# Top-k stage of a retrieval layer: a third of the subtractions on VectorE, transposes a token tile later, one-hots written in input order

## The chip, the cores and the metric

The kernel runs on one core of a Trainium2 chip. The metric is the device time of one execution in microseconds. Five engines work in parallel, each with its own queue that it takes strictly in order: TensorE (PE, matmuls; PEld is its weight load), VectorE (DVE), ScalarE (ACT), GpSimd (POOL) and SyncE (SP), which here only issues DMAs. They wait for one another by semaphores.

## The reference

A block of a small network on 256 tokens of width 1,024, in float32. Only its retrieval layer matters here: every token picks 128 of 16,384 experts (8 heads, top 16 of 256 candidates, which come from the top 16 of 128 sub-keys in each of two halves), and the outputs of the picked experts are summed by gate.

```python
def peer_ffn(xn, w_query, subkeys, u_tab, v_tab):
    q = (xt @ w_query).reshape(T, PEER_HEADS, 2, PEER_QDIM // 2)
    s = jnp.einsum('thpd,hpkd->thpk', q, subkeys).astype(jnp.float32)
    sv, si = lax.top_k(s, PEER_TOPK)
    cand = (sv[:, :, 0, :, None] + sv[:, :, 1, None, :]).reshape(T, PEER_HEADS, PEER_TOPK * PEER_TOPK)
    cand_id = (si[:, :, 0, :, None] * PEER_NKEYS + si[:, :, 1, None, :]).reshape(...)
    top_s, pos = lax.top_k(cand, PEER_TOPK)
    expert = jnp.take_along_axis(cand_id, pos, axis=-1)
    gate = jax.nn.softmax(top_s, axis=-1)
    def apply(args):
        ug, vg = u_tab[ec], v_tab[ec]
        act = jax.nn.gelu(jnp.einsum('thkd,td->thk', ug, xc).astype(jnp.float32), approximate=False)
        return jnp.einsum('thk,thkd->td', (gc * act).astype(vg.dtype), vg)
```

## The kernel before

Nothing is gathered. The kernel computes the activation of all 16,384 experts for all tokens, multiplies it with a dense matrix of gates, which is zero for experts not picked, and multiplies with the whole second table. So it streams both tables of 64 MB through TensorE.

**Weights.** Every product in float32 is made of three in a faster format. `wload` (L97 to 111) loads 128x1024 weights (`raw`, issued by SP), has ScalarE round them (`hi`, L106) and takes the rest `lo = raw - hi` (L109) on VectorE or GpSimd, as a pattern of letters says, which is walked round and round. There are 3 buffers of `raw`, 4 of `hi` and 4 of `lo`. `ws` (L242 to 262) then issues 24 matmuls for such a half: per block of 128 rows `hi` with the upper part of x (L255), `hi` with its lower part (L256) and `lo` with the upper part (L257). The 3rd matmul of a half is thus the first that wants its `lo`.

**Stages.** `peer` (L674 to 707) merges pairs of generators: it advances whichever has done the smaller share of its steps, so the number of steps that a generator announces sets how its instructions are written among those of the other. A scheduler then fixes the order on each engine. In the top-k stage `peer_topk` runs beside `peer_u` on the first half of the first table (64 halves, numbered from 0 here; pattern "G": every lo on GpSimd). For each tile of 128 tokens `peer_topk` computes the scores (16 products L749, recorded as 32), searches the 16 halves of heads (L755 to L759), makes candidates (L767), searches those of 8 heads (L772 to L776), and turns positions into expert numbers (L782 to L797: compare with 0..15, multiply, sum). Then come an Exp on ScalarE, the gate sums (L804 to L806) and three transposes on TensorE (L811 to L813), from which ScalarE makes `sel` and VectorE the copy `gate` (L815).

In the gates stage `peer_g` runs beside `peer_u` on the second half of the first table (pattern "VG"). For 8 tokens at a time VectorE compares the selected numbers with a ramp (`E`, L852, bf16, written as key x token), then for 4 tokens ScalarE copies one (`A`, L857) and VectorE multiplies the other by the gate (`B`, L858), both written as token x key in float32; 4 matmuls (L862, two records each) give the dense gates of 4 tokens, which multiply the activations there (L868) or are kept for later ones (L870). The last stage, `peer_v`, multiplies with the second table (L898), its lo's by the same pattern "VG".

Of the kernel before, what the change touches and what calls it, by code (L numbers as in the profile page):

```python
# [9 lines left out]
F32 = mybir.dt.float32  # L10
# [5 lines left out]
AF = mybir.ActivationFunctionType  # L16
ALU = mybir.AluOpType
AX = mybir.AxisListType
PSUM = bass.MemoryType.PSUM
P = 128  # L20
# [10 lines left out]
TOPK_STEPS = 90  # L31
# [14 lines left out]
class Net:  # L46
    def __init__(self, ctx, tc, T):
# [13 lines left out]
        self.u_pattern = "G"  # L61
# [667 lines left out]
    def peer_topk(self, qT, pool, sel, gate):  # L729
# [12 lines left out]
        nc.sync.dma_start(skT, T["subkeysT"])  # L742
        for tt in range(2):
# [9 lines left out]
            for hp in range(16):  # L753
                o, x = hp * 16, s[:, hp * P:(hp + 1) * P]
# [34 lines left out]
            for q in range(2):  # L789
# [7 lines left out]
                v.tensor_reduce(ij[:, q * P:(q + 1) * P], e3, axis=AX.X, op=ALU.add)  # L797
                yield

            self.tc.keep_in_program_order(a.activation(gt, gt, AF.Exp))  # L800
            for _ in range(2):
                yield
            sm = self.tiny.tile([P, 8], F32, tag="gsm", name=self.nm("gsm"))
            v.tensor_reduce(sm, g3, axis=AX.X, op=ALU.add)  # L804
            v.reciprocal(sm, sm)
            v.tensor_tensor(g3, g3, sm[:, :, None].to_broadcast([P, 8, 16]), op=ALU.mult)  # L806
            t = slice(tt * P, tt * P + P)
            for _ in range(2):
                yield
            p = self.sm_ps()  # L810
            nc.tensor.transpose(p[:, :P], ij[:, :P], self.ident)  # L811
            nc.tensor.transpose(p[:, P:2 * P], ij[:, P:], self.ident)
            nc.tensor.transpose(p[:, 2 * P:3 * P], gt, self.ident)  # L813
            a.activation(sel[:, :, t], p[:, :2 * P].rearrange("p (q t) -> p q t", q=2), AF.Copy)
            v.tensor_copy(gate[:, t], p[:, 2 * P:3 * P])  # L815

    def peer_u(self, xT, n0, n1):
# [16 lines left out]
        self.lo_pattern = self.u_pattern  # L834
        for x in g:
            yield x
            self.lo_pattern = self.u_pattern

    def peer_g(self, sel, gate, pool):
# [8 lines left out]
        for b in range(S // T1):  # L848
# [4 lines left out]
            for u in range(0, T1, T2):  # L853
                i = u // T2
                t0 = b * T1 + u
                A, B = [h[q].rearrange("p (n t j) -> p n t j", n=2, t=T2)[:, i] for q in range(2)]
                a.activation(A, E[0][:, :, u:u + T2].rearrange("p j t -> p t j"), AF.Copy)  # L857
                v.tensor_tensor(B, E[1][:, :, u:u + T2].rearrange("p j t -> p t j"),  # L858
                                gate[:, t0:t0 + T2, None].to_broadcast([P, T2, P]), op=ALU.mult)
                p = self.bank("sm").rearrange("p (t j) -> p t j", t=T2)  # L860
                for k in range(T2):
                    nc.tensor.matmul(p[:, k], A[:, k], B[:, k], start=True, stop=True)  # L862
# [618 lines left out]
```

## Time and profile before

| | |
|---|---|
| median of 3 runs | 1701.74 us (1701.32 to 1702.23) |
| the profiled execution | 1709.63 us, its span 1707.5 us, mean granted clock 0.985 |
| busy, share of the span | PE 97%, DVE 70%, ACT 55%, POOL 25% |
| top-k stage | 195 to 400 us |
| gates stage | 400 to 641 us |
| last product and end of the layer | 641 to 1010 us |

What stands outside 195 to 1010 us is the attention block ahead and two more layers behind. Busy TensorE records overlap and their ends are modelled, so the distance from one start to the next is the better measure of its pace. The clock is a share of full speed.

### The profile page before, as it was taken

To read this page: it belongs to the slowest core of one execution; us is meant where nothing else is said; L and a number is where in the kernel's file an instruction comes from. 1 tells how busy PE (TensorE), PEld (TensorE's weight loads), DVE (VectorE), ACT (ScalarE), POOL (GpSimd) and SP (SyncE) were. 2 spreads that over 40 slices of the span, in tenths; PEclk is the share of its full clock that TensorE was granted. 3 is DMA by queue.
4 is the path that set the end of the run, shared out by engine and by line. 5 is a ranking of instruction groups with operands and counts; after the bars stand their busy time and mean duration, and the time that the engine had idled before them with its cause. 6 is when DMAs were issued, how large, how long until landed. Compare 5 with 4: busy or idle time off the path is not lost.

```text
span 1707.5 us, 27637 instructions
## 1 busy us (share of the span) xinstructions
PE 1648.9 (97%) x10592; PEld 1467.1 (86%) x10592; DVE 1191.3 (70%) x2236; ACT 947.1 (55%) x1435; POOL 429.4 (25%) x191
## 2 busy tenths in 40 slices
PE   6999999989999999999999999989999989999998
PEld 5878999989999997888888879869998777799986
DVE  7766597915999995444444468878884685688845
ACT  4545545446676665555555557466664455566634
POOL 1000498974333334444444411100000000000000
PEclk9999999999999999999999999999999998999999
DMA  7424655555444446556755665436666642366661
GB/s 268 158 75 153 201 165 162 161 171 163 137 136 148 129 147 205 186 187 215 226 186 186 189 184 173 124 114 198 187 190 186 208 161 66 112 192 189 192 188 62
DMA packets 83200, 285.07 MB, mean 167 GB/s; under 512 B 10556, under 2 KB 14589, under 8 KB 82941
## 3 DMA queue, kind: packets, MB, share of 16 engines
q1 hardware_dynamic: 83068, 283.31, 53.4%
q8 instruction: 83, 1.36, 0.3%
q14 instruction: 49, 0.39, 0.1%
HBM read 281.16 MB, written 2.12 MB: 166 GB/s over the span
## 4 chain that ended last, share of the span: by engine, by line
PE 71%; DVE 23%; ACT 2%; issue 2%; DMA 1%; POOL 1%; SPq 0%; DVEq 0%; ACTq 0%; POOLq 0%
PE mm L898 20%; PE mm L256 9%; PE mm L257 9%; PE mm L255 9%; PE mm L196 6%; PE mm L198 6%; PE mm L197 6%; DVE h L858 6%; DVE lo L109 4%; DVE E L852 3%; DVE act L868 2%; PE sm L553 1%; PE sm L525 1%; DVE xn L322 1%; PE sm L334 1%
## 5 line engine op out<-in xcount | busy, mean ns | idle before, releaser
L106 ACT ACTIVATE hi<-raw 128x1024 fp32r<-128x1024 f32 x513 | 542.7, 1060 | 380.7 <-PE mm L256 141.4
L109 DVE TENSOR_TENSOR lo<-raw,hi 128x1024 fp32r<-128x1024 f32 x353 | 433.9, 1231 | 192.2 <-ACT hi L106 183.1
L255 PE MATMUL mm<-xTh,hi 128*128 128x256 f32 x1992 | 564.0, 283 | 0.1
L257 PE MATMUL mm<-xTh,lo 128*128 128x256 f32 x1992 | 557.0, 280 | 4.9 <-POOL lo L109 4.9
L256 PE MATMUL mm<-xTl,hi 128*128 128x256 f32 x1992 | 557.4, 280 | 0.4 <-DVE xTl L289 0.4
L109 POOL TENSOR_TENSOR lo<-raw,hi 128x1024 fp32r<-128x1024 f32 x160 | 405.7, 2541 | 426.4 <-ACT hi L106 416.7
L257 PEld LDWEIGHTS mm<-xTh,lo 128*128 128x128 f32 x1992 | 375.7, 189 | 6.1 <-POOL lo L109 5.9
L255 PEld LDWEIGHTS mm<-xTh,hi 128*128 128x128 f32 x1992 | 375.8, 189 | 1.3 <-issue 0.6
L256 PEld LDWEIGHTS mm<-xTl,hi 128*128 128x128 f32 x1992 | 375.9, 189 | 0.9 <-DVE xTl L289 0.7
L858 DVE TENSOR_TENSOR h<-E,gate 128x512 f32<-128x512 bf16 x64 | 115.2, 1800 | 4.2 <-PE sm L862 4.2
L196 PE MATMUL mm<-hi,xTh 128*128 128x512 f32 x256 | 107.6, 421 | 2.0 <-DVE xTl L289 1.0
L198 PE MATMUL mm<-hi,xTl 128*128 128x512 f32 x256 | 104.1, 408 | 2.2 <-DVE xTl L289 2.2
L197 PE MATMUL mm<-lo,xTh 128*128 128x512 f32 x256 | 104.7, 409 | 0.2 <-DVE lo L109 0.2
L289 DVE TENSOR_TENSOR xTl<-act,xTh 128x256 fp32r<-128x256 f32 x64 | 45.1, 713 | 80.3 <-PE mm L898 78.8
L289 DVE TENSOR_TENSOR wl<-act,wh 128x256 fp32r<-128x256 f32 x64 | 42.8, 675 | 82.9 <-PE mm L898 82.9
L857 ACT ACTIVATE h<-E 128x512 f32<-128x512 bf16 x64 | 73.1, 1143 | 40.9 <-DVE E L852 39.3
L1313 DVE SCALAR_TENSOR_TENSOR fc<-mm,cw,fc 128x255 f32<-128x255 f32 (+1 forms) x176 | 84.4, 480 | 3.1
L898 PE MATMUL mm<-hi,xTh 128*128 128x512 f32 x256 | 80.7, 396 | 0.9 <-DVE act L828 0.9
L898 PE MATMUL mm<-hi,xTl 128*128 128x512 f32 x256 | 80.6, 396 | 0.8 <-DVE xTl L289 0.8
L898 PE MATMUL mm<-lo,xTh 128*128 128x512 f32 x256 | 80.5, 395 | 0.0
L898 PE MATMUL mm<-hi,wl 128*128 128x512 f32 x256 | 80.2, 395 | 0.0
L898 PE MATMUL mm<-hi,wh 128*128 128x512 f32 x256 | 80.2, 395 | 0.0
(298 smaller groups left out, 2398.3 us busy)
## 6 DMA issues: line engine op xcount, KB each, us to landing
raw<-in_peer_uT SPq DMA_DIRECT2D x128, 512.0 KB, 3.7
raw<-in_peer_v SPq DMA_DIRECT2D x128, 512.0 KB, 4.4
raw<-in_ffn_up_ws SPq DMA_DIRECT2D x88, 512.0 KB, 4.3
raw<-in_ffn_down_a SPq DMA_DIRECT2D x40, 512.0 KB, 4.5
raw<-in_w_in_xs SPq DMA_DIRECT2D x20, 512.0 KB, 4.8
raw<-in_ab_ws SPq DMA_DIRECT2D x16, 512.0 KB, 4.5
raw<-in_ple_gate_xs SPq DMA_DIRECT2D x16, 512.0 KB, 4.3
raw<-in_w_query_ws SPq DMA_DIRECT2D x12, 512.0 KB, 5.0
```

Source lines behind the costliest of these rows:

```text
L106: nc.scalar.activation(hi, raw, AF.Copy)
L109: eng.tensor_tensor(lo, raw, f32(hi), op=ALU.subtract)
L196: nc.tensor.matmul(p, xh[:, k, t], hi[:, w], start=n == 1 and kk == 0, stop=False)
L197: nc.tensor.matmul(p, xh[:, k, t], lo[:, w], start=False, stop=False)
L198: nc.tensor.matmul(p, xl[:, k, t], hi[:, w], start=False, stop=n == total[c] and kk == 1)
L255: nc.tensor.matmul(o, hi[:, w], xh[:, k, :], start=k == 0, stop=False)
L256: nc.tensor.matmul(o, hi[:, w], xl[:, k, :], start=False, stop=False)
L257: nc.tensor.matmul(o, lo[:, w], xh[:, k, :], start=False, stop=k == 7)
L289: self.nc.vector.tensor_tensor(dl, p, f32(dh), op=ALU.subtract)
L858: v.tensor_tensor(B, E[1][:, :, u:u + T2].rearrange("p j t -> p t j"), gate[:, t0:t0 + T2, None].to_broadcast([P, T2, P]), op=ALU.mult)
L898: nc.tensor.matmul(self.acc[tt][c], st_[:, t], mv[:, c * 512:c * 512 + 512], start=first and j == js[0] and i == 0, stop=j == last and i == 2)
L1313: v.scalar_tensor_tensor(c[:, o + sft:o + S], p[:, o:o + S - sft], cw[:, wi, j:j + 1], c[:, o + sft:o + S], op0=ALU.mult, op1=ALU.add)
```

## The change

There are five parts. The lines from L31 on move by one or more, so the same operation has other line numbers behind the change: lo L110, the three matmuls of a half L256 to L258, score products L763, L792, L795 and L797 are L808, L811 and L813, transposes L753, `E` L857, `A` L863, `B` L864, gate products L867, last product L903.

1. The gate sums, the transposes and the copies behind them become a function `finish`. For tile 0 it is called in the middle of tile 1's search (at the 7th of 16), for tile 1 after 14 more steps. The Exp is issued after the first sum. The top-k stage announces 74 steps instead of 90.
2. The pattern of the top-k stage is "GGV": the lo's of halves 1, 4, 7, ..., 61 are VectorE's.
3. `A` and `B` are written in the order in which `E` lies. `A` keeps its place as token x key, so ScalarE writes in steps of 512 bytes; `B` becomes key x token, so that TensorE reads the moving operand of L867 in steps of 16 bytes.
4. Once 96 of the 128 blocks of activations are done, in the second half of the gates stage, the pattern is "VGG" instead of "VG".
5. `peer_u` leaves the pattern at "V", so the last product has all its lo's on VectorE.

```diff
-TOPK_STEPS = 90
+TOPK_STEPS = 74
+TOPK_REST = 14
-        self.u_pattern = "G"
+        self.u_pattern = "GGV"
+        def finish(tt, ij, gt, g3):
+            sm = self.tiny.tile([P, 8], F32, tag="gsm", name=self.nm("gsm"))
+            v.tensor_reduce(sm, g3, axis=AX.X, op=ALU.add)
+            v.reciprocal(sm, sm)
+            v.tensor_tensor(g3, g3, sm[:, :, None].to_broadcast([P, 8, 16]), op=ALU.mult)
+            p = self.sm_ps()
+            for i, x in enumerate((ij[:, :P], ij[:, P:], gt)):
+                self.tc.keep_in_program_order(nc.tensor.transpose(p[:, i * P:(i + 1) * P], x, self.ident))
+            t = slice(tt * P, tt * P + P)
+            a.activation(sel[:, :, t], p[:, :2 * P].rearrange("p (q t) -> p q t", q=2), AF.Copy)
+            v.tensor_copy(gate[:, t], p[:, 2 * P:3 * P])
...
             for hp in range(16):
+                if tt and hp == 6:
+                    finish(0, *late)
...
                 v.tensor_reduce(ij[:, q * P:(q + 1) * P], e3, axis=AX.X, op=ALU.add)
+                if not q:
+                    self.tc.keep_in_program_order(a.activation(gt, gt, AF.Exp))
                 yield
-            self.tc.keep_in_program_order(a.activation(gt, gt, AF.Exp))
...
+            late = ij, gt, g3
+        for _ in range(TOPK_REST):
+            yield
+        finish(1, *late)
...
-        self.lo_pattern = self.u_pattern
         for x in g:
+            self.lo_pattern = "VGG" if gates and self.done[0] >= 96 else self.u_pattern
             yield x
-            self.lo_pattern = self.u_pattern
+        self.lo_pattern = "V"
...
-                A, B = [h[q].rearrange("p (n t j) -> p n t j", n=2, t=T2)[:, i] for q in range(2)]
-                a.activation(A, E[0][:, :, u:u + T2].rearrange("p j t -> p t j"), AF.Copy)
-                v.tensor_tensor(B, E[1][:, :, u:u + T2].rearrange("p j t -> p t j"),
-                                gate[:, t0:t0 + T2, None].to_broadcast([P, T2, P]), op=ALU.mult)
+                A = h[0].rearrange("p (n t j) -> p n j t", n=2, t=T2)[:, i]
+                B = h[1].rearrange("p (n j t) -> p n j t", n=2, t=T2)[:, i]
+                a.activation(A, E[0][:, :, u:u + T2], AF.Copy)
+                v.tensor_tensor(B, E[1][:, :, u:u + T2], gate[:, None, t0:t0 + T2].to_broadcast([P, P, T2]), op=ALU.mult)
...
-                    nc.tensor.matmul(p[:, k], A[:, k], B[:, k], start=True, stop=True)
+                    nc.tensor.matmul(p[:, k], A[:, :, k], B[:, :, k], start=True, stop=True)
```

VectorE's queue at the end of tile 0, before: the last search, the comparison with 0..15 for both numbers, the multiplications and the sums.

```order
L776 MAX_INDEX small_2406<-small_2405,big_2403 128x8 x2
L782 TENSOR_TENSOR small_2634<-small_2405 128x128
L785 TENSOR_SCALAR small_2636<-small_2406 128x128
L786 TENSOR_SCALAR small_2636<-small_2406 128x128
L788 CAST small_2639<-small_2636 128x256
L792 TENSOR_TENSOR big_2641<-small_2639,io_1918 128x2048
L792 TENSOR_TENSOR big_2682<-small_2639,io_1918 128x2048
L795 TENSOR_TENSOR big_2641<-big_2641,small_2401 128x2048
L795 TENSOR_TENSOR big_2682<-big_2682,small_2401 128x2048
L797 TENSOR_REDUCE small_2633<-big_2641 128x128
L797 TENSOR_REDUCE small_2633<-big_2682 128x128
L804 TENSOR_REDUCE gsm_2774<-small_2634 128x8
```

The same place now, where lo_2550 is that of half 16, lo_2628 of half 19, and the next two of halves 22 and 25.

```order
L798 TENSOR_TENSOR small_2733<-small_2467 128x128
L804 CAST small_2738<-small_2735 128x256
L808 TENSOR_TENSOR big_2740<-small_2738,io_1918 128x2048
L808 TENSOR_TENSOR big_2807<-small_2738,io_1918 128x2048
L110 TENSOR_TENSOR lo_2550<-raw_2547,hi_2549 128x1024
L811 TENSOR_TENSOR big_2740<-big_2740,small_2463 128x2048
L811 TENSOR_TENSOR big_2807<-big_2807,small_2463 128x2048
L813 TENSOR_REDUCE small_2732<-big_2740 128x128
L110 TENSOR_TENSOR lo_2628<-raw_2625,hi_2627 128x1024
L813 TENSOR_REDUCE small_2732<-big_2807 128x128
L110 TENSOR_TENSOR lo_2774<-raw_2771,hi_2773 128x1024
L110 TENSOR_TENSOR lo_2846<-raw_2843,hi_2845 128x1024
```

Subtractions that had not been in this queue now stand between the operations of the top-k stage. In tile 1 they stand the same way: VectorE's queue there now, with lo_3474 that of half 40, lo_3552 of half 43 and lo_3698 of half 46 (those of halves 31, 34 and 37 stand among the searches).

```order
L857 TENSOR_TENSOR E_4277<-sel,iota 128x1024
L804 CAST small_3662<-small_3659 128x256
L864 TENSOR_TENSOR h_79<-E_4277,gate 128x512
L808 TENSOR_TENSOR big_3664<-small_3662,io_1918 128x2048
L110 TENSOR_TENSOR lo_3474<-raw_3471,hi_3473 128x1024
L811 TENSOR_TENSOR big_3664<-big_3664,small_3424 128x2048
L808 TENSOR_TENSOR big_3731<-small_3662,io_1918 128x2048
L813 TENSOR_REDUCE small_3656<-big_3664 128x128
L110 TENSOR_TENSOR lo_3552<-raw_3549,hi_3551 128x1024
L811 TENSOR_TENSOR big_3731<-big_3731,small_3424 128x2048
L864 TENSOR_TENSOR h_79<-E_4277,gate 128x512
L813 TENSOR_REDUCE small_3656<-big_3731 128x128
```

Behind the last row two more `E` and the lo of half 46 follow. On TensorE, before, the transposes of tile 0 and the score products of tile 1 stood together after half 22.

```order
L257 MATMUL mm_2778<-xTh_70,lo_2782 128x256
L811 MATMUL sm_2815<-ident,small_2633 128x128
L812 MATMUL sm_2815<-ident,small_2633 128x128
L813 MATMUL sm_2815<-ident,small_2634 128x128
L749 MATMUL sm_2822<-big_1920,qT_1436 128x128 x4
L749 MATMUL sm_2828<-big_1920,qT_1436 128x128 x4
```

Now the score products of tile 1 stand after half 24 and the transposes of tile 0 after half 29, as below; those of tile 1 stood after half 45 and stand after half 60.

```order
L258 MATMUL mm_3012<-xTh_70,lo_3022 128x256
L753 MATMUL sm_3083<-ident,small_2732 128x128 x2
L753 MATMUL sm_3083<-ident,small_2733 128x128
L256 MATMUL mm_3094<-xTh_70,hi_3097 128x256
L257 MATMUL mm_3094<-xTl_71,hi_3097 128x256
```

The transposes have moved away from the products that they stood ahead of, and back by 7 and by 15 halves.

## Rows read from the trace of the kernel before

**Rows 1.** Stages: window, its length, busy (x instructions) by engine, granted clock, DMA.

```profile
core 0: us, PE busy (x) PEld busy (x) DVE busy (x) ACT busy (x) POOL busy (x), PEclk, DMA share, GB/s
195.00:400.00 205.00, 192.34 (x1610) 190.89 (x1610) 139.35 (x423) 97.04 (x115) 173.19 (x64) 0.98 0.55 167
400.00:512.00 112.00, 112.00 (x971) 112.00 (x969) 104.02 (x145) 78.09 (x118) 35.04 (x16) 1.00 0.45 138
512.00:640.00 128.00, 127.14 (x1072) 124.67 (x1071) 127.75 (x165) 84.17 (x134) 40.25 (x17) 1.00 0.46 141
641.00:1010.00 369.00, 365.24 (x1564) 293.53 (x1563) 180.02 (x233) 195.30 (x273) 153.71 (x68) 1.00 0.63 196
```

**Rows 2.** What TensorE waited for, 195 to 400 us: total, times, longest.

```profile
PE sm L813 <- DVE small L806: 5.3, 1, 5.3
PE mm L257 <- POOL lo L109: 4.9, 5, 1.3
PE sm L749 <- DVE gate L815: 2.5, 1, 2.5
```

**Rows 3.** A window behind the longest of them, columns as in rows 1.

```profile
345.80:352.60 6.80, 5.80 (x27) 5.81 (x28) 1.23 (x2) 1.33 (x4) 3.17 (x2) 0.50 0.63 204
```

**Rows 4.** TensorE's timeline, start of the top-k stage: start, duration, operation.

```profile
195.28 3.73 PE L749 MATMUL sm<-big,qT 128*128 128x128 f32 x32
...
199.08 0.28 PE L257 MATMUL mm<-xTh,lo 128*128 128x256 f32 x1
...
201.88 0.28 PE L257 MATMUL mm<-xTh,lo 128*128 128x256 f32 x1
```

**Rows 5.** VectorE's timeline in the gates stage.

```profile
557.72 2.97 DVE L858 TENSOR_TENSOR h<-E,gate 128x512 f32<-128x512 bf16 x1
560.60 1.29 DVE L852 TENSOR_TENSOR E<-sel,iota 128x1024 bf16<-128x1024 bf16 x2
...
562.55 1.06 DVE L858 TENSOR_TENSOR h<-E,gate 128x512 f32<-128x512 bf16 x1
...
563.77 1.22 DVE L109 TENSOR_TENSOR lo<-raw,hi 128x1024 fp32r<-128x1024 f32 x1
```

**Rows 6.** VectorE's timeline in the top-k stage, tile 0.

```profile
198.06 0.49 DVE L755 MAX8 small<-big 128x8 f32<-128x128 f32 x2 [10.87 <-ACT big L751]
...
216.77 2.28 DVE L767 TENSOR_TENSOR big<-small 128x2048 f32<-128x2048 f32 x1
218.96 0.29 DVE L762 CAST small<-small 128x256 f32<-128x256 uint32 x1
...
235.06 2.38 DVE L788 CAST small<-small 128x256 f32<-128x256 uint32 x1
237.47 8.90 DVE L792 TENSOR_TENSOR big<-small,io 128x2048 f32<-128x2048 f32 x2
246.29 8.88 DVE L795 TENSOR_TENSOR big<-big,small 128x2048 f32<-128x2048 f32 x2
255.09 4.47 DVE L797 TENSOR_REDUCE small<-big 128x128 f32<-128x2048 f32 x2
```

**Rows 7.** GpSimd by line, 240 to 262 us, then 400 to 641: busy, mean ns, idle.

```profile
L109 POOL TENSOR_TENSOR lo<-raw,hi 128x1024 fp32r<-128x1024 f32 x6 | 22.0, 3707 | 0.3 <-ACT hi L106 0.3
...
L109 POOL TENSOR_TENSOR lo<-raw,hi 128x1024 fp32r<-128x1024 f32 x33 | 79.2, 2400 | 168.6 <-ACT hi L106 159.2 <-PE mm L257 5.2 <-ACT act L870 4.2
```

**Rows 8.** By line, 400 to 641; line L830 (min/median/max ns); a VectorE row of 646 us.

```profile
L857 ACT ACTIVATE h<-E 128x512 f32<-128x512 bf16 x62 | 70.9, 1143 | 38.7 <-DVE E L852 37.1 <-PE mm L257 1.6
...
L862 PE MATMUL sm<-h,h 128*128 128x128 f32 x512 | 68.6, 277 | 0.9 <-DVE h L858 0.3
...
L830 ACT ACTIVATE act<-mm x63: 186/577/618, 207.0 to 639.5; 128x512 f32<-128x512 f32 x32, 128x496 f32<-128x496 f32 x1, 128x480 f32<-128x480 f32 x1, 128x464 f32<-128x464 f32 x1
...
646.12 0.68 DVE L828 TENSOR_TENSOR act<-mm,act 128x512 f32<-128x512 f32 x1
```

**Rows 9.** What TensorE waited for, 536 to 650 us.

```profile
PE mm L898 <- DVE act L828: 0.9, 1, 0.9
PE mm L898 <- DVE xTl L289: 0.8, 1, 0.8
```

More of the change, by code (lines that the diff above doesn't have):

```diff
@@ L797, in peer_topk @@
                 v.tensor_reduce(ij[:, q * P:(q + 1) * P], e3, axis=AX.X, op=ALU.add)
+                if not q:
+                    self.tc.keep_in_program_order(a.activation(gt, gt, AF.Exp))
                 yield
-            self.tc.keep_in_program_order(a.activation(gt, gt, AF.Exp))
[L801 to L815, printed above, removed]
+            late = ij, gt, g3
+        for _ in range(TOPK_REST):
+            yield
+        finish(1, *late)
     def peer_u(self, xT, n0, n1):
```

## Prediction

> **What bounds the kernel now.** I read the busy time by stage first, then what TensorE waited for, then the timelines of the engines that it waited for. Four stages matter, and TensorE is busy nearly all the time in each [rows 1]: the top-k stage (195 to 400 us: 192.34 of 205), the gates stage in two parts (112.00 of 112, then 127.14 of 128), and the last product (365.24 of 369). So work that leaves VectorE, ScalarE or GpSimd is worth only the time that TensorE waits, and work that arrives there costs nothing until TensorE has to wait for it. In the top-k stage it waits 12.7 us in all: 5.3 for a transpose (L813) whose input VectorE has not written, 4.9 in five waits for a lo that GpSimd is late with, 2.5 for the gate copy that holds a PSUM bank [rows 2]. The long stop has a sequel: for 6.80 us after it the granted clock is 0.50, the lower level, with TensorE busy 5.80 of them [rows 3], so about 2.9 us more are lost. The change can win at most 15.6 us here.
>
> **Pace of the top-k stage.** TensorE takes 2.80 us for a half of 1,024 weight columns, from one first use of lo to the next (199.08 to 201.88), and 0.117 us for each of the 32 records of a score product (3.73 us); the first product starts at 195.28 [rows 4]. I count the halves of this stage from 0: half n wants its lo at 199.08 + 2.80n, plus whatever was waited.
>
> **Part 1: gate sums and transposes later.** The operations are the same. The transposes of tile 0 now stand after half 29 and those of tile 1 after half 60 in TensorE's queue, where VectorE has written their inputs long before, and the score products of tile 1 no longer stand behind the gate copy. That removes 5.3 + 2.5 + 2.9 = 10.7 us. Next late in their place are the lo's.
>
> **Part 2: every third lo of the top-k stage on VectorE.** 21 of 64 leave GpSimd. The cost is not 21 x 1.22 us [rows 5] but where they stand: VectorE is an in-order queue and top-k fills it. Before, nothing that TensorE wants half by half was in that queue.
>
> Tile 0: VectorE starts at 198.06 and finishes its two L792 at 246.29 (the start of L795) [rows 6], and in the new order the lo's of halves 4, 7, 10 and 13 stand ahead of that point and that of half 16 right behind it. Its lo is ready at 246.29 + 5 x 1.22 = 252.4 and wanted at 199.08 + 16 x 2.80 = 243.9: 8.5 us late. That is with the durations of before, and those contain GpSimd. L792 and L795 take 4.45 each, two operands in SBUF and 2,048 elements, where L767 of the same size took 2.28 [rows 6]; beside them GpSimd's lo took 3.71 instead of 2.40 [rows 7]. They take turns. So the lower end has L792 at 2.28 (-4.3) and the cast L788 at 0.29 as L762 instead of 2.38 (-2.1): 2.1 us late. For half 19, two L795, one L797 (half of 4.47) and a lo come next: 8.0 us alone or 12.4 as before, against 8.4 of three halves. By the end of tile 0 TensorE has waited 2.1 to 12.5 us.
>
> Tile 1: VectorE starts 2.78 us after the first score product [rows 4, 6], and half 25 wants its lo 3.80 us after it. Half 40 wants its lo 15 halves and three transposes later, at 3.80 + 42.0 + 0.35 = 46.2. Ahead of it stand the 16 sub-key searches (18.71), L767 (2.19), the gate copy and a cast (0.3 each), the candidate searches up to L788 (235.06 - 218.96 = 16.1), two E at 0.65, one gated one-hot at 1.06 [rows 5], an L792 (2.28) and four lo's with its own (4.9): 2.78 + 47.1 = 49.9, 3.7 late. With L788 and L792 as before it is 8.0. Half 43 takes L795, L792, L797 and lo (8.0 to 12.4) and half 46 L795, L797, a gated one-hot, two E and lo (8.1 to 12.2), each against 8.4. So TensorE waits 3.7 to 15.8 us in tile 1.
>
> Together 5.8 to 28.3. Where between depends on how often VectorE meets GpSimd. GpSimd keeps two of three subtractions, so I take two thirds of the way, 20.8, and 1.2 for meetings of the new lo's themselves (ten of them, each 0 to 2.2 more; up to 2 at the upper end): 22. A stop of more than 5 us is likely once, with its slow clock after it as in [rows 3]: 3 more (0 to 6). The stage: 22 + 3 - 12.7 - 2.9 = **+9.4**; ends -10 and +21.
>
> **Part 3: one-hots in input order.** ScalarE's copy reads E with a stride of 16 bytes and takes 1.14 us, where a copy of 512 elements in a row takes 0.58 [rows 8]; VectorE's multiplication takes 1.06, where L828 on 512 takes 0.68 [rows 5, 8]. So about 0.4 us per four tokens leave VectorE, and some 0.5 ScalarE, if ScalarE's spread write is free. What they bring is TensorE's waiting only: 0 of 112 and 0.86 of 128 us [rows 1], with small slips between products, 2 at most. The price of the other side, a moving operand read at a stride of 16 bytes, no row shows. Its lower bound is 0, since the columns are as many; its upper bound is the rival below. I take 0: the record of 128 columns takes 0.117 us, 0.9 ns a column, half the pace at which L257 takes its 256 columns (0.117 too) [rows 4], so there is room.
>
> The Trainium skill, "SBUF - State Buffer", section Specifications, has 16-byte lines in SBUF and asks for two hits on a line for full bandwidth. That speaks for the change on ScalarE and VectorE, as these rows do, and against it on TensorE, whose every column is now a new line; the sum would be +9 without that penalty and that of the second rival with it.
>
> **Part 4: second half of the gates stage, two thirds of its lo's to GpSimd.** VectorE there is busy 127.75 of 128 us [rows 1], but part of that is waiting: the same multiplication takes 2.97 or 1.06 us [rows 5] by whether a GpSimd lo stands in its way. It loses a third of a lo per period and gains a third of a meeting. With part 3: 0, between -2 and +4.
>
> **Part 5: all lo's of the last product on VectorE.** 64 more, 78 us, in a stage where it is busy 180.02 of 369 and TensorE is never short of work [rows 1]: 0, hidden by the products; uncovered it would be 78. At the switch TensorE waits 0.9 and 0.8 us for VectorE [rows 9]; I take half a microsecond off that (0 to 1.7).
>
> **Sum.** 9.4 + 0 - 0.5 = +8.9 us. The profiled execution takes 1709.63 us, of which 1707.5 is the span, and would become 1718.5. The median of the runs shown is 1701.74, 7.9 below it, and the sum carries over as it stands: 1710.7.
>
> **Rivals.**
> First, **faster: VectorE hardly meets GpSimd any more.** Then the durations alone hold: 5.8 us of new waits, no slow clock, against 15.6 gone, 2 from the gates and 1.7 at the switch: -13.5, 1688 us. For it: L767 met nothing at 2.28, and two thirds of the subtractions are two thirds of the meetings at most. Against it: GpSimd was busy 21.92 of 22.00 us beside L792 and L795 (six at 3.71) [rows 7], and its remaining lo's come just there. Between this and my forecast the sums cancel, at 1702.
> Second, **slower still: TensorE pays for the stride.** Per element the strided reads of [rows 5, 8] cost 0.74 ns more on VectorE and 1.1 on ScalarE. On 128 columns and 512 records [rows 8] that is 49 to 72 us, all on a bound engine: 1760 to 1783 with the rest. It decides as soon as one column takes more than the 0.9 ns it has. For it: both engines that read so show it. Against it: none of them is TensorE.
> Third, the change **doesn't do what it says**: the transposes still wait. Against that stand 15 halves, 42 us, by which tile 1's move back; I give it nothing of its own.
>
> **Chances.** Forecast (new waits eat the gain, 1705 to 1726): 0.40. Cancelling, within 0.2%, which is about what a measurement of this kernel can tell from no change: 0.16. Faster, 1688 to 1698: 0.29. Stride on TensorE: 0.15. So faster 0.29, same 0.16, slower 0.55. The range leaves out the last case and the tails: 1688 to 1726, the upper end being 28.3 + 2 + 6 - 15.6 + 4 = +25. Cases of both signs hold much of the chance; the forecast's own range is 1705 to 1726.
>
> **What would show it.** In the changed profile: no wait of a transpose for VectorE; waits of L258 for VectorE's lo at halves 16, 19, 40, 43 and 46, some 20 us, perhaps with the clock at 0.50 behind one. L808 and L811 (L792, L795 now) at 2.3 us would be the first rival, records of the gate product above 0.117 us the second. The copy near 0.6 and the multiplication near 0.7 us would confirm part 3. I am wrong if the top-k stage comes out shorter than 205 us.

## The result, and the profile of the changed kernel

The changed kernel takes 1757.89 us (median of 6 runs) against 1701.99 of the kernel before (also 6): 1.0324 times as long, with an interval from 1.0304 to 1.0344. Slower, as forecast, but by 56 us where 9 were forecast, and outside the range. It is the second rival, to which the prediction gave 0.15.

The stages by TensorE's starts show where the time is. The top-k stage runs from the first score product to the first gate product, the gates stage to the last gate product.

| us | before | after | difference |
|---|---|---|---|
| top-k stage | 204.7 | 207.1 | +2.4 |
| gates stage | 238.4 | 294.3 | +55.9 |
| switch, last product | 362.9 | 360.7 | -2.2 |
| the rest | 901.5 | 896.7 | -4.8 |
| span | 1707.5 | 1758.8 | +51.3 |

The rest holds the same work in both. It begins up to 6 us earlier or later from run to run of any of the kernels here, and nothing is made of it.

The windows of the changed kernel, with the columns of [rows 1]: the top-k stage, then 230 us of the gates stage.

```profile
195.00:400.00 205.00, 191.22 (x1581) 189.66 (x1581) 143.20 (x429) 94.77 (x112) 115.69 (x42) 0.97 0.50 163
...
470.00:700.00 230.00, 230.00 (x1576) 221.48 (x1576) 154.82 (x244) 130.53 (x204) 68.30 (x29) 1.00 0.37 120
```

TensorE is busy all of those 230 us, and VectorE only 154.82, where before it was busy 127.75 of 128 [rows 1]. Nothing keeps TensorE waiting there (the list of its waits, below, has none in this stage), so TensorE itself is slower. Its timeline shows at what: start, duration and operation around one step of four tokens.

```profile
522.93 0.28 PE L258 MATMUL mm<-xTh,lo 128*128 128x256 f32 x1
523.05 1.98 PE L867 MATMUL sm<-h,h 128*128 128x128 f32 x8
524.66 0.48 PE L256 MATMUL mm<-xTh,hi 128*128 128x256 f32 x1
524.98 0.28 PE L257 MATMUL mm<-xTl,hi 128*128 128x256 f32 x1
```

The same place in the kernel before:

```profile
556.88 1.05 PE L862 MATMUL sm<-h,h 128*128 128x128 f32 x8
557.69 0.36 PE L255 MATMUL mm<-xTh,hi 128*128 128x256 f32 x1
557.89 0.28 PE L256 MATMUL mm<-xTl,hi 128*128 128x256 f32 x1
```

From the first record of a step to the second matmul behind it passes 1.93 us instead of 1.01. The ends of records are modelled, so this distance of starts is what counts; the median of all 64 steps is 1.935 against 1.013. The added 0.922 us on 64 steps are 59.0 us (57.8 when the 64 steps are added up one by one), and the stage grew by 55.9. Where the other 2 to 3 us were saved stays open: before, the list of waits has only 0.3 us in this stage. The start-to-start distance of two records rose from 0.112 to 0.227 us in the median.

The groups of the changed kernel (busy, mean ns of one, idle before) answer to [rows 8]:

```profile
L867 PE MATMUL sm<-h,h 128*128 128x128 f32 x512 | 126.5, 403 | 0.0
...
L863 ACT ACTIVATE h<-E 128x512 f32<-128x512 bf16 x64 | 74.2, 1162 | 49.1 <-PE sm L867 41.3
```

ScalarE's copy did not get cheaper: 1.162 us against 1.143. It now reads in runs of four and writes in steps of 512 bytes. VectorE's multiplication did, to 0.679 us at its fastest (line L864: minimum, median and maximum of 64).

```profile
L864 DVE TENSOR_TENSOR h<-E,gate x64: 679/1493/2316, 319.6 to 683.7; 128x512 f32<-128x512 bf16 x64
```

From 195 to 720 us TensorE's waits are these, all of them in the top-k stage; they answer to [rows 2]:

```profile
PE mm L258 <- DVE lo L110: 10.0, 5, 5.6
PE mm L258 <- POOL lo L110: 3.5, 1, 3.5
PE mm L256 <- ACT hi L107: 0.3, 1, 0.3
```

The transposes and the gate copy hold nothing up any more, and VectorE's lo's do, as forecast, for half as long. The slow clock has not gone: it comes twice, from within the stop of 5.6 us on and around that of 3.5 us (columns as in [rows 3]).

```profile
244.10:250.80 6.70, 3.76 (x17) 3.76 (x18) 6.70 (x3) 0.00 (x0) 1.80 (x1) 0.50 0.41 109
329.40:336.10 6.70, 5.82 (x27) 5.82 (x28) 6.70 (x4) 0.00 (x0) 4.18 (x2) 0.50 0.39 133
```

Half of TensorE's busy time in them, as the prediction reckoned it, is 4.8 us, against 2.9 before. Waits of 13.8 and these 4.8, less the 12.7 and 2.9 of before, give +3.0 us for the stage; it measured +2.4.

### The profile page after: what moved, and what is told of

It is laid out like the page before. It is cut to its first block, busy times and chain, and to the rows that moved or that the text cites. A ratio compares the mean times of both kernels' runs of the same rounds, so it can differ in the third digit from the quotient of the medians.

```text
span 1758.8 us, 27633 instructions
## 1 busy us (share of the span) xinstructions
PE 1702.5 (97%) x10592; PEld 1514.2 (86%) x10592; DVE 1199.9 (68%) x2315; ACT 952.4 (54%) x1435; POOL 233.1 (13%) x112
## 4 chain that ended last, share of the span: by engine, by line
PE 85%; DVE 10%; DMA 1%; issue 1%; ACT 1%; POOL 0%; SPq 0%; DVEq 0%; ACTq 0%; POOLq 0%
PE mm L903 20%; PE mm L258 12%; PE mm L256 12%; PE mm L257 12%; PE sm L867 7%; PE mm L197 6%; PE mm L199 6%; PE mm L198 6%; DVE lo L110 3%; PE sm L554 1%; PE sm L526 1%; PE sm L335 1%; DVE xn L323 1%; PE sm L1133 1%; PE sm L538 1%
## 5 line engine op out<-in xcount | busy, mean ns | idle before, releaser
L110 DVE TENSOR_TENSOR lo<-raw,hi 128x1024 fp32r<-128x1024 f32 x432 | 537.3, 1245 | 252.9 <-ACT hi L107 248.0
L256 PE MATMUL mm<-xTh,hi 128*128 128x256 f32 x1992 | 572.4, 288 | 0.4 <-ACT hi L107 0.3
L258 PE MATMUL mm<-xTh,lo 128*128 128x256 f32 x1992 | 559.5, 281 | 13.5 <-DVE lo L110 10.0
L257 PE MATMUL mm<-xTl,hi 128*128 128x256 f32 x1992 | 557.5, 280 | 0.4 <-DVE xTl L290 0.4
L258 PEld LDWEIGHTS mm<-xTh,lo 128*128 128x128 f32 x1992 | 376.5, 189 | 14.9 <-DVE lo L110 11.0
L256 PEld LDWEIGHTS mm<-xTh,hi 128*128 128x128 f32 x1992 | 377.7, 190 | 3.0 <-issue 0.6
L257 PEld LDWEIGHTS mm<-xTl,hi 128*128 128x128 f32 x1992 | 377.8, 190 | 2.1 <-DVE xTl L290 0.7
L110 POOL TENSOR_TENSOR lo<-raw,hi 128x1024 fp32r<-128x1024 f32 x81 | 209.4, 2590 | 319.0 <-ACT hi L107 296.1
L867 PE MATMUL sm<-h,h 128*128 128x128 f32 x512 | 126.5, 403 | 0.0
L873 DVE TENSOR_TENSOR act<-sm,act 128x256 f32<-128x256 f32 x126 | 42.2, 356 | 101.1 <-PE sm L867 97.5
L867 PEld LDWEIGHTS sm<-h,h 128*128 128x128 f32 x512 | 99.4, 203 | 7.5
L863 ACT ACTIVATE h<-E 128x512 f32<-128x512 bf16 x64 | 74.2, 1162 | 49.1 <-PE sm L867 41.3
L864 DVE TENSOR_TENSOR h<-E,gate 128x512 f32<-128x512 bf16 x64 | 80.6, 1260 | 5.2 <-PE sm L867 5.2
L903 PE MATMUL mm<-hi,xTh 128*128 128x512 f32 x256 | 80.8, 396 | 0.0
L903 PE MATMUL mm<-hi,xTl 128*128 128x512 f32 x256 | 80.8, 395 | 0.0
L903 PE MATMUL mm<-lo,xTh 128*128 128x512 f32 x256 | 80.8, 395 | 0.0
L903 PE MATMUL mm<-hi,wl 128*128 128x512 f32 x256 | 80.2, 395 | 0.0
```

The source lines that it names most:

```text
L110: eng.tensor_tensor(lo, raw, f32(hi), op=ALU.subtract)
L256: nc.tensor.matmul(o, hi[:, w], xh[:, k, :], start=k == 0, stop=False)
L257: nc.tensor.matmul(o, hi[:, w], xl[:, k, :], start=False, stop=False)
L258: nc.tensor.matmul(o, lo[:, w], xh[:, k, :], start=False, stop=k == 7)
L864: v.tensor_tensor(B, E[1][:, :, u:u + T2], gate[:, None, t0:t0 + T2].to_broadcast([P, P, T2]), op=ALU.mult)
L867: nc.tensor.matmul(p[:, k], A[:, :, k], B[:, :, k], start=True, stop=True)
```

## Experiments

The open questions were whether the stride alone makes the 56 us, why parts 1 and 2 cost less than forecast, and what the other parts do. Durations of stages are read as above.

| kernel | ratio to before, interval | top-k stage | gates stage |
|---|---|---|---|
| before | 1 | 204.7 | 238.4 |
| after: all parts | 1.0324, 1.0304 to 1.0344 | 207.1 | 294.3 |
| e1: without part 3 | 1.0131, 1.0069 to 1.0194 | 212.2 | 253.5 |
| e2: part 3 alone | 1.0327, 1.0249 to 1.0405 | 201.0 | 292.6 |
| e3: all, B in rows | 1.0105, 1.0038 to 1.0171 | 212.1 | 250.7 |
| e4: A alone, loaded in steps | 1.0325, 1.0264 to 1.0386 | 205.2 | 296.2 |
| e5: B in steps of 8 bytes | 0.9954, 0.9920 to 0.9989 | 199.9 | 235.2 |
| e6: B in steps of 32 bytes | 1.0327, 1.0263 to 1.0391 | 202.0 | 295.6 |
| e7: part 1 alone | 0.9999, 0.9966 to 1.0032 | 205.7 | 238.3 |
| e8: parts 1, 2, 5 | 1.0010, 0.9972 to 1.0048 | 211.9 | 238.0 |
| e9: e7, copy held back | 0.9939, 0.9912 to 0.9966 | 198.3 | 238.0 |
| e10: e9 and e5's B | 0.9919, 0.9888 to 0.9951 | 196.6 | 232.8 |
| e11: e8, copy held back | 1.0046, 1.0019 to 1.0073 | 220.2 | 236.0 |
| e12: e10 with A in steps of 8 | 0.9901, 0.9861 to 0.9940 | 194.9 | 234.9 |

### e1 and e2: the layout taken away, and the layout alone

e1 puts the old layout back into the changed kernel:

```diff
-                A = h[0].rearrange("p (n t j) -> p n j t", n=2, t=T2)[:, i]
-                B = h[1].rearrange("p (n j t) -> p n j t", n=2, t=T2)[:, i]
-                a.activation(A, E[0][:, :, u:u + T2], AF.Copy)
...
+                A, B = [h[q].rearrange("p (n t j) -> p n t j", n=2, t=T2)[:, i] for q in range(2)]
+                a.activation(A, E[0][:, :, u:u + T2].rearrange("p j t -> p t j"), AF.Copy)
...
```

> The changed kernel with part 3 alone undone: A and B token x key as before, both operands of the gate product read in a row. Theory (the stride of TensorE's moving operand costs the time): each record of the gate product is back from 0.201 us to 0.117 us, the gates stage from 294 to about 238 us, and the whole at 1695 to 1708 us, against 1758. Rival (the subtractions given to GpSimd in the second half of the gates stage, or VectorE's fuller queue, cost it): the gates stage stays above 280 us and the whole above 1740.

e2 makes the same edit the other way round in the kernel before.

> The kernel before with part 3 alone added. Theory (stride): 64 steps of 8 records, each 0.084 us longer, and a slower first matmul behind each step: +50 to +58 us, 1752 to 1760, the top-k stage unchanged at 205 us. Rival (the other parts cost it): 1697 to 1705, since A and B are cheaper on their engines.

e2 settles the main question: part 3 alone costs 1.0327, as much as all parts together. Its gates stage is at 292.6 us, its records start 0.227 us apart, and a step takes what it takes in the changed kernel:

```profile
525.38 1.98 PE L862 MATMUL sm<-h,h 128*128 128x128 f32 x8
526.99 0.48 PE L255 MATMUL mm<-xTh,hi 128*128 128x256 f32 x1
527.31 0.28 PE L256 MATMUL mm<-xTl,hi 128*128 128x256 f32 x1
```

The top-k stage, expected unchanged at 205 us, came out at 201.0. In e1 the records are back at 0.112, but the kernel is not back at the time of before: 1.013 instead of about 1. The gates stage keeps 15 of the 56 us, which neither theory had. TensorE's waits in e1 from 530 to 665 us name VectorE's multiplication:

```profile
PE sm L867 <- DVE h L863: 14.5, 15, 1.7
```

VectorE's groups in e1 from 530 to 640 us (busy, mean ns, idle before):

```profile
L863 DVE TENSOR_TENSOR h<-E,gate 128x512 f32<-128x512 bf16 x26 | 34.9, 1342 | 0.0
L857 DVE TENSOR_TENSOR E<-sel,iota 128x1024 bf16<-128x1024 bf16 x26 | 32.2, 1278 | 6.2 <-ACT h L862 6.2
L110 DVE TENSOR_TENSOR lo<-raw,hi 128x1024 fp32r<-128x1024 f32 x8 | 18.5, 2316 | 0.0
```

And in the kernel before, the same window:

```profile
L858 DVE TENSOR_TENSOR h<-E,gate 128x512 f32<-128x512 bf16 x28 | 54.1, 1933 | 0.0
L109 DVE TENSOR_TENSOR lo<-raw,hi 128x1024 fp32r<-128x1024 f32 x15 | 18.2, 1212 | 0.0
L852 DVE TENSOR_TENSOR E<-sel,iota 128x1024 bf16<-128x1024 bf16 x28 | 17.8, 675 | 0.0
```

Before, GpSimd's lo stood in the way of the multiplication alone. In e1 it meets `E` and VectorE's own lo as well, which take 0.6 and 1.1 us more on average, and 26 multiplications fit where 28 did. The lo's of VectorE became fewer and cost as much (8 for 18.5 us, 15 for 18.2). The windows of this stretch (columns of [rows 1]), before and then e1:

```profile
530.00:640.00 110.00, 109.14 (x918) 106.93 (x918) 109.75 (x144) 72.05 (x114) 33.69 (x14) 1.00 0.45 140
530.00:640.00 110.00, 97.31 (x817) 95.13 (x816) 102.56 (x124) 64.83 (x103) 43.97 (x17) 1.00 0.39 125
```

For each multiplication VectorE is busy 3.92 us before and 3.94 in e1: what two thirds of the lo's on GpSimd took off it, the meetings used up. What e1 adds is 7.4 us in which VectorE stands idle, 6.2 of them in front of `E`, waiting for ScalarE's copy. That a longer `E` delays the copy, and the copy the next `E`, is likely but not shown. Whether part 4 is behind all this is e8's question.

### e3 and e4: who pays for which stride

e3 keeps B token x key in the changed kernel, so VectorE reads in runs and writes in steps of 512 bytes:

```diff
-                B = h[1].rearrange("p (n j t) -> p n j t", n=2, t=T2)[:, i]
+                B = h[1].rearrange("p (n t j) -> p n j t", n=2, t=T2)[:, i]
...
```

> The changed kernel with B kept token x key: VectorE still reads E in runs of four and writes in steps of 512 bytes, as ScalarE does for A, and TensorE reads the moving operand in a row. Theory (stride of the moving operand): records at 0.117 us and the whole where the first run of this call is, 1695 to 1708. The multiplication shows whether a spread write costs what a spread read did: 0.68 us if it is free, 1.05 or more if it costs the same. Rival: above 1740.

e4 changes A alone in the kernel before: key x token, so that the stationary operand is loaded in steps of 16 bytes.

```diff
+                A = h[0].rearrange("p (n j t) -> p n j t", n=2, t=T2)[:, i]
+                a.activation(A, E[0][:, :, u:u + T2], AF.Copy)
...
+                    nc.tensor.matmul(p[:, k], A[:, :, k], B[:, k], start=True, stop=True)
```

> The kernel before with A alone in the order of E, so that the stationary operand is loaded at a stride of 16 bytes and the moving one read in a row. If TensorE pays for every new 16 bytes whatever it reads them for, the load of 128 columns grows like the moving read, by 0.084 us in each of 512 records, up to +43 us where it isn't hidden behind the product ahead (1702 to 1745). If it pays only for the moving operand: 1700 to 1703. ScalarE's copy then writes in a row and should fall from 1.14 to 0.6 us.

e3's records are at 0.112 us, and its time, 1.0105, is that of e1 within the intervals. Its multiplication takes 1.015 us at its fastest: a spread write costs VectorE what a spread read did. e4 shows that this holds for ScalarE's copy too, and it shows a third place of this price, the weight load (minimum, median, maximum ns of 512):

```profile
L863 PEld LDWEIGHTS sm<-h,h x512: 309/330/332, 394.6 to 690.9; 128*128 128x128 f32 x171
...
L858 ACT ACTIVATE h<-E x64: 632/633/637, 267.4 to 682.1; 128x512 f32<-128x512 bf16 x64
```

The load takes 0.330 us where 0.19 is usual, records start 0.233 us apart instead of 0.112, the step takes 1.98 us instead of 1.013, and the ratio is that of the moving operand, 1.0325. That is above both ranges of the expectation, whose price of 0.084 us a record was too low. The longer load is not hidden behind a product whose moving operand lies in a row; whether one behind a longer product would be, no run shows, since none has both operands spread. ScalarE's copy, which reads in runs of four and writes in a row, falls to 0.633 us, of which nothing arrives.

### e5 and e6: the step itself

e5 pairs tokens in B of the kernel before, so that TensorE reads in steps of 8 bytes, and VectorE reads `E` in runs of two and writes in a row:

```diff
+                B = h[1].rearrange("p (n m j t) -> p n m j t", n=2, m=T2 // 2, t=2)[:, i]
...
+                v.tensor_tensor(B, E[1][:, :, u:u + T2].rearrange("p j (m t) -> p m j t", m=T2 // 2),
+                                gate[:, t0:t0 + T2].rearrange("p (m t) -> p m t", t=2)[:, :, None, :].to_broadcast([P, T2 // 2, P, 2]), op=ALU.mult)
...
+                    nc.tensor.matmul(p[:, k], A[:, k], B[:, k // 2, :, k % 2], start=True, stop=True)
```

> The kernel before with B laid out so that two tokens alternate: TensorE reads the moving operand in steps of 8 bytes, two columns from each 16 bytes; A as before. If what costs is a new 16 bytes for every column, two columns share them and the record stays at or near 0.112 us: 1692 to 1705. If the cost grows with the step itself or any step costs: half the added 0.115 us of the 16-byte step or all of it, 1718 to 1760.

e6 interleaves eight tokens, steps of 32 bytes:

```diff
+                B = h[1].rearrange("p (j n t) -> p j n t", n=2, t=T2)[:, :, i]
...
```

> The kernel before with B of eight tokens interleaved: TensorE reads the moving operand in steps of 32 bytes, A as before. If the cost is one per new 16 bytes, it is that of the 16-byte step: records at 0.227 us, +3.3% (1745 to 1762). If it grows with the step, the records go on to 0.3 us or more and the whole above 1790.

One step of e5, and its multiplication:

```profile
523.46 1.07 PE L863 MATMUL sm<-h,h 128*128 128x128 f32 x8
524.28 0.37 PE L255 MATMUL mm<-xTh,hi 128*128 128x256 f32 x1
524.49 0.28 PE L256 MATMUL mm<-xTl,hi 128*128 128x256 f32 x1
...
L859 DVE TENSOR_TENSOR h<-E,gate x64: 672/681/2773, 308.0 to 618.2; 128x512 f32<-128x512 bf16 x64
```

The step takes 1.03 us (1.013 before), and the multiplication 0.672 us at its fastest: runs of two are enough for VectorE and all but enough for TensorE. e5 has VectorE's share of part 3's gain without the price, 0.9954: the gates stage is 3.2 us shorter than before, the top-k stage 4.8. e6 costs what 16 bytes cost, 1.0327 with 1.98 us a step. So the price is absent at 8 bytes and the same at 16 and 32, which fits one payment per new 16 bytes.

A count agrees. At 16 and 32 bytes a record touches 128 such pieces in 0.227 and 0.233 us, 1.8 ns each; in e5 it touches 64 of them in 0.114 us, again 1.8. In a row it touches only 32, in 0.112 us, so there the columns set its pace, 0.9 ns each. A record of L257 reads 256 columns of 4 bytes in a row, 64 pieces in 0.117 us [rows 4]. That is 1.8 ns a piece too, but whether pieces or columns set its pace no run tells: before the run it gave only an upper bound for the price of a piece.

The Trainium skill, "SBUF - State Buffer", section Specifications, asks for at least two hits on a 16-byte line for full bandwidth. e5 and e6 agree for TensorE's moving operand, with 0.114 us at two hits and 0.233 at one.

### e7 and e8: the parts without the layout

e7 is part 1 alone (the pattern stays "G", layouts and the other patterns as before). e8 is e1 without part 4:

```diff
-            self.lo_pattern = "VGG" if gates and self.done[0] >= 96 else self.u_pattern
+            self.lo_pattern = self.u_pattern
```

> The kernel before with part 1 alone: gate sums, transposes and copies later, every lo of the top-k stage on GpSimd, layouts and the other patterns as before. Theory: the wait of the transposes (5.3 us), that for the gate copy (2.5) and the slow clock (2.9) go and nothing comes in their place but GpSimd's waits (4.9): the top-k stage 194 to 197 us instead of 204.7, the whole 0.5 to 0.7% faster. Rival: TensorE catches up with GpSimd, which is the slower one beside L792 and L795, and waits there for what it has won: within 0.2%.

> The kernel of e1 (parts 1, 2, 4, 5) without part 4: the lo's of the whole gates stage alternate between VectorE and GpSimd as before. Theory: the 15 us by which that stage grew in e1 (253.5 against 238.4) are the two thirds on GpSimd, which stand in the way of VectorE's operations; the stage goes back to 238 to 240 and the whole to 1.005 to 1.007 of before, what is left being the top-k stage (212.2 against 204.7). Rival: it is the order that the new finish gives to the gates stage; then the stage stays near 253 and the whole at 1.013.

e8 bears out its theory: the gates stage is at 238.0 again. The whole is 1.0010 instead of 1.013, below the 1.005 expected, which is just outside its interval. Part 4 costs 15 us with the old layout. In the changed kernel it cost little that shows (the gates stage takes 294.3 us there, and 292.6 in e2, which has none of parts 1, 2, 4 and 5). The likely reason is that TensorE was so slow that VectorE, busy 154.82 of 230 us, had time. What is left of parts 1, 2 and 5 is 7.2 us more in the top-k stage.

e7 came out at the rival's number, but neither the theory nor the rival had the main reason. No transpose waits, yet nothing is won. TensorE's waits of e7 from 180 to 720 us:

```profile
PE mm L258 <- POOL lo L110: 11.3, 2, 10.0
PE mm L256 <- ACT hi L107: 1.8, 1, 1.8
...
```

ScalarE's timeline in e7 (start, duration, operation, and in brackets the idle time before and what ended it):

```profile
299.69 1.06 ACT L107 ACTIVATE hi<-raw 128x1024 fp32r<-128x1024 f32 x1 [2.32 <-DMA raw<-in_peer_uT]
308.52 2.15 ACT L862 ACTIVATE h<-E 128x512 f32<-128x512 bf16 x2 [7.77 <-DVE E L857]
310.58 1.04 ACT L107 ACTIVATE hi<-raw 128x1024 fp32r<-128x1024 f32 x1
```

GpSimd's, beside it:

```profile
300.83 2.40 POOL L110 TENSOR_TENSOR lo<-raw,hi 128x1024 fp32r<-128x1024 f32 x1 [0.42 <-ACT hi L107]
311.70 28.67 POOL L110 TENSOR_TENSOR lo<-raw,hi 128x1024 fp32r<-128x1024 f32 x8 [8.47 <-ACT hi L107]
```

The wait list names GpSimd, but GpSimd sat 8.47 us waiting for a hi. ScalarE sat 7.77 us in front of the first one-hot copy of the gates stage, which the scheduler had put into the middle of the top-k stage and whose `E` stands on VectorE behind tile 1's searches. The hi's of the next halves stood behind it. Before, `sel` of tile 0 was ready early and its first `E` stood ahead of these searches; part 1 moved `sel` back, `E` with it, and ScalarE's copy met the gap. The changed kernel has the same stop, 7.42 us at 318.04:

```profile
318.04 2.13 ACT L863 ACTIVATE h<-E 128x512 f32<-128x512 bf16 x2 [7.42 <-DVE E L857]
```

### e9 to e12: the copy held back

e9 adds one thing to e7: the copies of the first block keep their place in program order, behind the hi's of the top-k stage.

```diff
-                a.activation(A, E[0][:, :, u:u + T2].rearrange("p j t -> p t j"), AF.Copy)
+                (self.tc.keep_in_program_order if b == 0 else (lambda x: x))(a.activation(A, E[0][:, :, u:u + T2].rearrange("p j t -> p t j"), AF.Copy))
```

> The kernel of e7 (part 1 alone) with the first two one-hot copies of ScalarE (L862) held back in its queue to where they are written, behind the hi's of the top-k stage. In e7 ScalarE sat 7.8 us before them, waiting for VectorE's E, with the next hi's behind them, and TensorE then waited 10.3 us for a lo. Theory (that copy, at the head of an in-order queue, is what ate part 1's gain): the wait falls from 11.3 us to GpSimd's own 3 to 5, the top-k stage to 194 to 198 us, the whole to 0.993 to 0.996 of before. Rival (GpSimd itself is late beside L808 and L811): the wait stays near 10 us and the whole within 0.2%.

e10 is e9 with e5's B, e11 is e8 with the same copies held back.

> The kernel of e9 with B in pairs of tokens as in e5 (TensorE's moving operand in steps of 8 bytes), which was 0.995 of before alone. The gains lie in different stages, e9's in the top-k stage, e5's in the gates stage (235.2 against 238.4 us) and part of the switch, so they should add: 0.988 to 0.993. If the two only moved the same wait, no better than the better of them, 0.995.

> The kernel of e8 (parts 1, 2 and 5) with the same two copies held back. Against e9 it differs by every third lo of the top-k stage on VectorE (and the last product's lo's). Theory of the prediction (those lo's are late because top-k stands ahead of them): TensorE still waits 10 to 14 us for VectorE's lo at halves 13, 16, 40 and 43, the stage is 8 to 14 us longer than e9's, the whole 0.998 to 1.004 of before. Rival (e8's waits were the copy's, too): the stage is as short as e9's and the whole 0.993 to 0.996.

e9's waits from 185 to 720 us:

```profile
PE sm L867 <- ACT h L862: 4.4, 1, 4.4
PE mm L258 <- POOL lo L110: 3.4, 3, 1.3
...
```

The theory holds: GpSimd's wait falls from 11.3 to 3.4 us, the stage to 198.3, and 0.9939 is what part 1 is worth without the stop. Holding back costs 4.4 us itself, once, at the first gate product. In e10 the ratio, 0.9919, lies where it was expected if the two gains add, and the two stages together are 6.9 us shorter than in e9 (196.6 and 232.8 us). But its interval, 0.9888 to 0.9951, holds e9's 0.9939 too, so the ratio does not settle that they add. e11 differs from e9 by the thirds on VectorE (and the last product, 1 us shorter), and its wait list from 185 to 720 us says what they cost:

```profile
PE mm L258 <- DVE lo L110: 21.6, 7, 7.7
...
PE sm L867 <- ACT h L862: 0.5, 1, 0.5
```

The top-k stage is 21.9 us longer than e9's, and the whole is at 1.0046; the theory had 8 to 14 us and at most 1.004. The waits make 14.3 of the 21.9 (22.1 against 7.8), and the granted clock is at 0.50 for 20.5 us in this stage, against none in e9's ahead of the first gate product. Not all of it is the pattern's: the held-back copy also changed VectorE's order, and in e11 the lo of half 43 stands behind all four of L808 and L811, where in e8 it stood behind two and one. e8, in its own order, waited 13.1 us for VectorE's lo's.

e12 pairs A as well:

```diff
-                A = h[0].rearrange("p (n t j) -> p n t j", n=2, t=T2)[:, i]
+                A = h[0].rearrange("p (n m j t) -> p n m j t", n=2, m=T2 // 2, t=2)[:, i]
...
+                    nc.tensor.matmul(p[:, k], A[:, k // 2, :, k % 2], B[:, k // 2, :, k % 2], start=True, stop=True)
```

> The kernel of e10 with A in pairs of tokens too: TensorE loads the stationary operand in steps of 8 bytes. If two columns per 16 bytes are enough for the load as they are for the moving operand (e4 had 330 ns a load at 16 bytes, 190 in a row), the load stays at 188 to 192 ns and the whole within 0.3% of e10's 0.992; ScalarE's copy, with writes and reads in runs of two, falls from 1.14 us towards the 0.63 of e4. If the load pays at 8 bytes, some 20 us more, 1.003.

```profile
L863 ACT ACTIVATE h<-E x64: 644/668/691, 383.9 to 618.0; 128x512 f32<-128x512 bf16 x64
...
L868 PEld LDWEIGHTS sm<-h,h x512: 193/197/201, 390.3 to 625.0; 128*128 128x128 f32 x171
```

The load takes 0.197 us (0.19 in a row, 0.192 the upper end of what was expected), the copy 0.668, the step 1.063 us, and the ratio 0.9901 has e10's 0.9919 inside its interval. e10 and e12 are both faster than the kernel before, by 0.8 and 1.0%; which of the two is better is not settled.

## Why the prediction was wrong

**What failed is one term, the price of the moving operand's stride (part 3).** The prediction took 0 and priced the rival at 49 to 72 us; 64 steps of 0.922 us more are 59.0. The step that failed is the reason for the 0: it compared columns (0.9 ns a column against half of that for L257) and found room. By 16-byte pieces there was none: at a stride of 16 bytes every column is a piece, and a piece takes 1.8 ns (e2, e6), twice the 0.9 ns that a column had. L257 takes four columns from each piece, so its pace allowed a price of up to 1.8 ns a piece and showed no room. The mechanism stood in the text, in the rows of two engines, and was put aside because no row was TensorE's. The rule of two hits on a line, which the prediction cites from the Trainium skill, "SBUF - State Buffer", section Specifications, says the same, and e5 and e6 bear it out. With an unknown price between 0 and 72 us on a bound engine, and the nearest rows at the upper end, the value to take was theirs.

**That the sign was right is luck.** The forecast's own reason, new waits in the top-k stage, brought +2.4 us of the 56. Without part 3 the kernel comes out inside the forecast's range (e1, 1.0131), but by the wrong terms: 7.5 us in the top-k stage and 15 from part 4, which the sum had at 0.

**Part 3's gain was sized half right.** VectorE's multiplication went to 0.68 us as its row said. ScalarE's copy did not: the condition "if ScalarE's spread write is free" was false (1.162 us; 1.015 on VectorE in e3). The gain was put at 2 us at most, all of it in the gates stage. Without the price it is larger: e5's two stages are 8.0 us shorter than before, 4.8 of that in the top-k stage, and e10's 6.9 shorter than e9's, 1.7 of that in the top-k stage (one profile of each).

**Part 1 was right in what it removes, wrong in what comes next.** The waits of 5.3 and 2.5 us are gone, as the wait list of after shows. The slow clock behind the first is not won: it came back behind other stops. The prediction named the lo's as next late, and did not follow the moved transposes on to what reads `sel`: `E` on VectorE and the copy on ScalarE, with the hi's behind it. e7 and e9 show this: 205.7 us with the stop, 198.3 without, against 204.7.

**Part 2 was right in kind.** New waits for VectorE's lo's, in both tiles, come to 10.0 us in the changed kernel, 13.1 in e8 and 21.6 in e11; the sum took 22 between 5.8 and 28.3. They came earlier than it said: at halves 10, 13 and 16 (0.6, 1.1 and 5.6 us) and at 37 and 40 (0.6 and 2.1). Of the five halves that it named, 19, 43 and 46 did not wait. In the changed kernel VectorE met GpSimd less often than two thirds of the time, as the groups from 195 to 400 us show:

```profile
L808 DVE TENSOR_TENSOR big<-small,io 128x2048 f32<-128x2048 f32 x4 | 11.3, 2840 | 0.0
L811 DVE TENSOR_TENSOR big<-big,small 128x2048 f32<-128x2048 f32 x4 | 11.2, 2828 | 0.0
```

They take 2.84 us in the mean instead of 4.47; at 2.28 alone and 2.2 a meeting that is one meeting in four. GpSimd's timeline in the same trace shows why:

```profile
254.38 4.98 POOL L110 TENSOR_TENSOR lo<-raw,hi 128x1024 fp32r<-128x1024 f32 x2 [8.47 <-PE mm L257]
...
322.04 11.54 POOL L110 TENSOR_TENSOR lo<-raw,hi 128x1024 fp32r<-128x1024 f32 x2 [7.49 <-ACT hi L107]
```

Beside tile 0's L811 (246.9 to 251.4) GpSimd stood idle, by this row for TensorE, which had itself stood before VectorE's lo of half 16. In tile 1 it first waited for ScalarE's stopped hi's, and then it was GpSimd that lost: two of its lo's took 11.54 us instead of 4.8. The sum had no wait for GpSimd any more; TensorE waited 3.5 us for its lo of half 41.

The top-k stage came out at +2.4 us (forecast +9.4); in e8, with the old layout, at +7.2. By waits (15.5 us against 13.8) and by half of TensorE's busy time at the clock of 0.50 (8.2 against 4.8) the traces account for these 5 us. Most of them come from one place: e8 waits 3.4 us for the lo of half 34, with the slow clock around it, and the changed kernel does not. Ahead of that lo VectorE's queue in e8 has

```profile
289.39 3.27 DVE L110 TENSOR_TENSOR lo<-raw,hi 128x1024 fp32r<-128x1024 f32 x1
...
300.50 2.29 DVE L778 CAST small<-small 128x256 f32<-128x256 uint32 x1
```

and the changed kernel, in the same order, takes 1.24 and 0.29 us for these two. In e8 GpSimd's lo had begun 0.21 us before the first of them, in the changed kernel 0.02 us after it. No one-hot multiplication had run in this stage by then (the first starts at 319.6 us), so its lower cost is not the cause. e1 and e3 have the stage at 212 as e8 has, so chance alone is not likely either; what shifts the two engines against each other stays open.

**Part 4 was sized too low.** 0 between -2 and +4 was forecast; with the old layout it costs 15 (e1 against e8), and in the changed kernel it is likely covered by TensorE's slowness. The prediction set a third of a lo against a third of a meeting; e1 shows that the meetings moved from one operation to three, and that VectorE then also stood idle for ScalarE's copy.

**Part 5 was right:** nothing of the 78 us arrives. That the last product takes 357.6 us against 359.9 is not its doing: e2, without part 5, has 357.6 too. The switch takes 3.1 against 3.0, so the half microsecond put on it did not come.

## What to carry to other kernels

Before an operand is laid out for the engine that writes it, count the 16-byte pieces that each reader takes from it. Here a record of 128 columns took the longer of two times, 0.9 ns for each column or 1.8 ns for each piece, and pairs of 4-byte elements were enough to keep both sides fast. When a step is moved back, follow its result through every queue to the first instruction that stands ahead of bound work, and look in the wait list for an engine that is named as late while it waits itself. A part that costs nothing in one version can be covered by another part's damage: part 4 showed its 15 us only when the stride was gone.

## What the runs showed of the hardware

TensorE paid for a step of 16 or 32 bytes between 4-byte columns: 0.227 and 0.233 us a record against 0.112 in a row. For a weight load at 16 bytes it was 0.330 against 0.19 us, with records 0.233 us apart. At 8 bytes the records took 0.114 us (e5) and the load 0.197 (e12). VectorE and ScalarE paid alike for reading 2-byte elements in steps of 16 bytes and for writing 4-byte elements in steps of 512: 1.05 (read) and 1.02 (write) against 0.68 us for a multiplication at its fastest, 1.14 and 1.16 against 0.63 us for a copy. Writes in steps of 16 bytes were not run. A VectorE operation on two operands of 2,048 elements took 2.28 us alone and 4.5 beside GpSimd's lo. In the two meetings compared under part 2 the engine that began later lost, in the changed kernel by 0.02 us.
